# A streaming encoder layer on one core: the first modulation with weight blocks as the stationary operand

## The chip, the cores and the metric

One core of a Trainium2 chip runs the whole program. The metric is the device time of one execution in microseconds (us); lower is better.

## The reference

One layer of a hybrid encoder is applied to a prompt (512 tokens) and to a sample (64 tokens). What this case touches is the adaptive modulation at its start; the rest is cut.

```python
def trunk(x, c, states, params, block):
    ...
    mod = jax.nn.silu(c) @ w_ada[l] + b_ada[l]          # c: one row of 2048, for prompt and for sample
    sh1, sc1, g1, sh2, sc2, g2 = jnp.split(mod[:, None, :], N_MOD, axis=-1)
    h = rmsnorm(x, norm1[l]) * (1 + sc1) + sh1
    mix, ... = token_mixers(h, ..., w_in[l], ...)       # h @ w_in, two recurrences, out projection
    x = x + g1 * mix
    h = rmsnorm(x, norm2[l]) * (1 + sc2) + sh2
    f, s_f = conv_ffn(h, ...)
    x = x + g2 * f
```

All data are f32. `w_ada` is 2048 x 12288, six parts of 2048 columns; the first part is `sh1`, the second `sc1`. The head of the kernel needs these two only: a product of two rows (the prompt's c and the sample's) with 2048 x 4096 weights, 33.6 MB.

## The kernel before

**How it multiplies.** Large products are made from operands split in a high and a low half (tiles of type F32R): the high half is a rounded copy made by ScalarE (ACT, L649), the low half the rest, a subtraction on VectorE (DVE, L650). `wtile` loads a 512 KB tile of weights into `raw` or `hraw` over SyncE's queue (SP) and splits it to `wh` and `wl`. A wide product is three matmuls: high by high, low by high, high by low (`mm6`, L561 and L563), here with 128x128 weights stationary and 288 columns of the activations moving.

**The head.** `head` turns x to channel-major by TensorE transposes (L698), computes the rows' norms and their scaling (L725, L726), and makes the modulation of four 128-channel blocks at a time: `modulation(g)` for g = 0 to 3, each for `sc1` (mi = 1) and then `sh1` (mi = 0). So there are eight modulations of 2048 x 512 weights, each of eight tiles with two k (128 rows) in a tile. `modulation(0)` comes first, with the loads, turns and norms of x between its tiles. Then, for each g, `modulation(g + 1)` comes ahead of the work on the four blocks of g: their modulated h (`split_mod`), the narrow product (L877), and the first q and k products (L561 and L563 on `g` and `ps_k`, 64 wide matmuls per g with the narrow ones). TensorE keeps this order; the head ends with the last of these products. Behind it come the projections, the recurrences, the output projection and the FFN.

**The modulation before.** The columns of silu(c) are the stationary operand and the weights move, 512 columns at a time. `cst` holds for each k the high halves of both c's and the low halves (4 columns), padded with zeros to NW = 66. For six of the eight tiles the weights are split, and each k has two matmuls, by `wh` (L757) and by `wl` (L758). For the tiles at k0 = 4 and 12 the raw f32 weights move past the unsplit columns `cs4` (L753). The result lies in four rows of 512 columns; DVE copies it (`rw`, L760), four small matmuls (L763) turn it to columns and add the high and low rows, and `put_mod` adds the bias (L797).

The later modulations (parts 2 to 5) are made on VectorE by `ada_block`, whose sums are turned by matmuls with 128x128 stationary sums and one moving column (L826). These are not changed.

Of the kernel before, what the change touches and what calls it, by code (L numbers as in the profile page):

```python
# [8 lines left out]
F32 = mybir.dt.float32  # L9
F32R = mybir.dt.float32r  # L10
I32 = mybir.dt.int32
AF = mybir.ActivationFunctionType
ALU = mybir.AluOpType
# [3 lines left out]
P = 128  # L17
D = 2048
KD = 16
# [28 lines left out]
NW = 66  # L48
# [53 lines left out]
class Kern:  # L102
# [554 lines left out]
    def head(self, pool):  # L657
        nc, i = self.nc, self.i
        V, A, T = nc.vector, nc.scalar, nc.tensor
# [2 lines left out]
            next(vectors)  # L662

        self.ct = self.cp.tile([P, 2, KD], F32, name="ct")
        cst = pool.tile([P, KD, NW], F32R, tag="cst", bufs=1, name="cst")
        nc.gpsimd.memset(cst.bitcast(F32), 0.0)
        for s in range(2):
            A.activation(self.ct[:, s], self.vmap[f"c{s}"], AF.Silu)
        cs4 = pool.tile([P, KD, 4], F32, tag="cs4", bufs=1, name="cs4")
        nc.gpsimd.memset(cs4, 0.0)  # L670
        for s in range(2):
            V.tensor_copy(cs4[:, :, s], self.ct[:, s])
            A.activation(cst[:, :, s], self.ct[:, s], AF.Copy)
            V.tensor_tensor(cst[:, :, 2 + s], self.ct[:, s], cst[:, :, s].bitcast(F32), op=ALU.subtract)
        self.mod = self.cp.tile([P, 6, KD, 2], F32, name="mod")
# [61 lines left out]
        def hraw():  # L737
            if next(turns) == "r":
                return self.raw()
            return pool.tile([P, 1024], F32, tag="hraw", bufs=5, name=self.name("hraw"))  # L740

        def modulation(g, between=lambda: None):
            for mi in (1, 0):
                ps = self.bank()
                c0 = mi * D + g * 512
                for k0 in range(0, KD, 2):
                    between()
                    src = i["w_ada"][0, k0 * P:(k0 + 2) * P, c0:c0 + 512].rearrange("(k p) n -> p k n", p=P)
                    if k0 in (4, 12):
                        raw = hraw().rearrange("p (k n) -> p k n", k=2)  # L750
                        nc.sync.dma_start(raw, src)
                        for k in range(2):
                            T.matmul(ps[:4], cs4[:, k0 + k], raw[:, k], start=False, stop=False)  # L753
                        continue
                    wh, wl = self.wtile(src, hraw())
                    for k in range(2):
                        T.matmul(ps[:NW], cst[:, k0 + k], wh[:, k], start=(k0 + k == 0), stop=False)  # L757
                        T.matmul(ps[:NW], cst[:, k0 + k], wl[:, k], start=False, stop=(k0 + k == KD - 1))  # L758
                rw = pool.tile([4, 512], F32, tag="rw", bufs=1, name=self.name("rw"))
                V.tensor_copy(rw, ps[:4])  # L760
                pc = self.bank()
                for j in range(4):
                    T.matmul(pc[:, 2 * j:2 * j + 2], rw[:, j * P:(j + 1) * P], self.c["sel"][:4, 16:18], start=True, stop=True)  # L763
                self.put_mod(mi, 4 * g, pc)
                for _ in vectors:
                    pass
            self.scale_mod(s1, 1, "norm1", 4 * g)

        plan = [[] for _ in range(16)]
        for b in range(5):  # L770
            for f, at in ((x_load, 0), (x_turn, X_LAG), (x_norm, X_LAG + 1)):
                plan[X_AT[b] + at].append(lambda f=f, b=b: f(b))
        step = iter(plan)
        modulation(0, lambda: [f() for f in next(step)])
        rx = x_rows()
        self.ps_nar, self.ps_q0 = self.pgt(), self.pgt()
        for g in range(4):
            if g < 3:
                modulation(g + 1)
            ks = range(4 * g, 4 * g + 4)  # L780
            nar = self.narrow_w(pool, 4 * g)
            qw, kw = [self.split(pool, self.w_in(off)(4 * g, 4 * g + 4), "f", 512, 3) for off in (OFF_BQ, OFF_BK)]
            for k in ks:
                hh, hl = self.htiles(k)
                tmp = pool.tile([P, 2, HT], F32, tag="tmp", bufs=2, name=self.name("tmp"))
                self.split_mod(xT[:, k], rx, s1[:, k], self.mod[:, 0, k], hh, hl, tmp)
                nc.sync.dma_start(self.xs[k], xT[:, k])
                self.h.append((hh, hl))
                self.mm_narrow(k, nar[:, k % 4])
                for ps, w in ((self.ps_q0, qw), (ps_k0, kw)):  # L790
                    self.mm6(ps, w[0][:, k % 4], w[1][:, k % 4], self.h[k], k == 0, k == KD - 1)
        raw = self.xr()
        self.ps_k0 = raw[:, :2 * HT].rearrange("p (h t) -> p h t", h=2)
        V.tensor_copy(self.ps_k0, ps_k0[:, :, :HT])

    def put_mod(self, mi, k0, pc):
        self.nc.vector.tensor_tensor(  # L797
            self.mod[:, mi, k0:k0 + 4], pc[:, :8].rearrange("p (j s) -> p j s", s=2),
            self.vec("b_ada", mi * KD + k0, 4).unsqueeze(2).to_broadcast([P, 4, 2]), op=ALU.add)

    def scale_mod(self, out, mi, norm, k0, n=4):

# [1188 lines left out]
```

## Time and profile before

| | |
|---|---|
| time, median of 3 runs | 2870.66 us (2866.38 to 2871.43) |
| the profiled execution's own time | 2869.18 us |
| its span, first to last instruction | 2867.4 us |
| mean granted TensorE clock | 0.992 |
| TensorE (PE) busy | 2810.4 us, 98% |
| weight loads (PEld) busy | 2708.7 us, 94% |
| VectorE (DVE), ScalarE (ACT), GpSimd (POOL) busy | 80%, 47%, 11% |
| DMA | 399.80 MB, mean 139 GB/s |

PE and PEld are the two sides of TensorE: matmuls and the loads of their stationary operands, which overlap. A matmul's record contains its latency, so successive records overlap, and the distance of their starts tells the rate. The granted clock is the share of full speed that TensorE's clock was given. In a list of instructions "idle before <-X" is how long the engine stood still ahead of them and what ended that. Groups give busy time and the mean length of one in ns. A plain f32 matmul leaves two records, one of F32R operands one.

### The profile page before, as it was taken

What the parts mean: (1) busy time and instruction counts of PE and PEld (TensorE: products, weight loads), DVE (VectorE), ACT (ScalarE), POOL (GpSimd) and SP (SyncE); (2) the same over time, 40 slices, a digit from 0 to 9 for tenths busy, and PEclk for the clock granted to TensorE, in tenths of its full rate; (3) what the DMA queues carried; (4) which work ended last, traced back from release to release, by engine and by line L of the source; (5) the groups of instructions that cost most, each with busy time, mean ns of one, the idle gap of its engine ahead of it and who ended that gap; (6) DMA issues with size and microseconds to landing.
All of it is one profiled execution on the core that took longest, in us unless ns stands there. A gap on an engine that the chain in (4) does not pass through costs nothing.

```text
span 2867.4 us, 52042 instructions
## 1 busy us (share of the span) xinstructions
PE 2810.4 (98%) x20596; PEld 2708.7 (94%) x20596; DVE 2301.9 (80%) x3742; ACT 1355.0 (47%) x2379; POOL 320.6 (11%) x587
## 2 busy tenths in 40 slices
PE   7999999999999999999999999999999999999998
PEld 3599999999999999999999999999999999999997
DVE  5788878777778777468888888888887889999995
ACT  7574566544333333255444444444444464434453
POOL 0005432224310001001000000000000000000000
PEclk9999999999999999999999999999999999999999
DMA  9975555545455448433333333333333343443451
GB/s 308 306 209 148 157 149 161 158 140 152 129 166 172 146 131 251 123 119 102 102 101 102 108 106 108 102 108 108 101 101 105 105 150 114 123 127 118 126 169 67
DMA packets 522441, 399.80 MB, mean 139 GB/s; under 512 B 50793, under 2 KB 453956, under 8 KB 522196
## 3 DMA queue, kind: packets, MB, share of 16 engines
q1 hardware_dynamic: 516772, 385.79, 45.3%
q0 software_dynamic: 5424, 10.68, 1.2%
q8 instruction: 162, 2.65, 0.4%
q14 instruction: 83, 0.68, 0.1%
HBM read 356.24 MB, written 40.13 MB: 138 GB/s over the span
## 4 chain that ended last, share of the span: by engine, by line
PE 82%; DVE 9%; DMA 3%; ACT 3%; issue 2%; SPq 0%; POOL 0%; ACTq 0%; DVEq 0%
PE g L561 19%; PE g L563 10%; PE g L1373 9%; PE g L1374 8%; PE g L1375 8%; PE bank L1374 3%; PE bank L1373 3%; PE bank L1375 3%; DVE wl L1558 2%; PE g L1606 2%; PE g L1608 2%; PE g L1607 2%; DMA raw<-in_w_down_dram 1%; PE bank L162 1%; PE bank L826 1%
## 5 line engine op out<-in xcount | busy, mean ns | idle before, releaser
L1373 PE MATMUL g<-slot,wh 128*128 128x290 f32 x1760 | 534.2, 304 | 2.4 <-ACT p L1385 2.4
L1374 PE MATMUL g<-slot,wh 128*128 128x290 f32 x1760 | 526.6, 299 | 0.0
L1375 PE MATMUL g<-slot,wl 128*128 128x290 f32 x1760 | 520.9, 296 | 0.0
L561 PE MATMUL g<-hh,wh 128*128 128x288 f32 x1984 | 450.4, 307 | 2.4 <-ACT hh L1160 1.3
L561 PE MATMUL g<-hl,wh 128*128 128x288 f32 x1984 | 432.3, 298 | 0.0
L563 PE MATMUL g<-hh,wl 128*128 128x288 f32 x1984 | 432.0, 298 | 0.0
L1320 ACT ACTIVATE wh<-raw 128x1024 fp32r<-128x1024 f32 x176 | 186.8, 1061 | 393.1 <-PE g L1374 376.8
L1373 PEld LDWEIGHTS g<-slot,wh 128*128 128x128 f32 x1760 | 331.8, 189 | 16.9 <-ACT p L1385 11.3
L1375 PEld LDWEIGHTS g<-slot,wl 128*128 128x128 f32 x1760 | 337.2, 192 | 0.0
L1374 PEld LDWEIGHTS g<-slot,wh 128*128 128x128 f32 x1760 | 335.6, 191 | 0.1
L561 PEld LDWEIGHTS g<-hh,wh 128*128 128x128 f32 x1984 | 319.1, 190 | 5.6 <-ACT hh L1160 1.5
L561 PEld LDWEIGHTS g<-hl,wh 128*128 128x128 f32 x1984 | 321.3, 189 | 0.3
L563 PEld LDWEIGHTS g<-hh,wl 128*128 128x128 f32 x1984 | 319.6, 189 | 0.2 <-issue 0.2
L649 ACT ACTIVATE wh<-raw 128x1024 fp32r<-128x1024 f32 x163 | 172.6, 1059 | 309.1 <-PE g L561 272.6
L650 DVE TENSOR_TENSOR wl<-raw,wh 128x1024 fp32r<-128x1024 f32 x163 | 199.1, 1222 | 52.8 <-ACT wh L649 50.9
L820 DVE SCALAR_TENSOR_TENSOR acc<-xr,ct,acc 128x512 f32<-128x512 f32 x322 | 230.4, 751 | 1.5 <-DMA xr<-in_w_ada_dram 1.5
L1321 DVE TENSOR_TENSOR wl<-raw,wh 128x1024 fp32r<-128x1024 f32 x176 | 214.8, 1220 | 19.3 <-ACT wh L1320 19.2
L1606 PE MATMUL g<-slot,wh 128*128 128x288 f32 x760 | 224.8, 296 | 2.3 <-DVE slot L1623 1.1
L1608 PE MATMUL g<-slot,wl 128*128 128x288 f32 x760 | 224.4, 296 | 0.3 <-DVE wl L1558 0.3
L1607 PE MATMUL g<-slot,wh 128*128 128x288 f32 x760 | 224.4, 295 | 0.0
L1374 PE MATMUL bank<-slot,wh 128*128 128x290 f32 x704 | 210.3, 299 | 0.0
L1373 PE MATMUL bank<-slot,wh 128*128 128x290 f32 x704 | 209.6, 298 | 0.0
(416 smaller groups left out, 6083.0 us busy)
## 6 DMA issues: line engine op xcount, KB each, us to landing
raw<-in_w_up_dram SPq DMA_DIRECT2D x176, 512.0 KB, 4.0
raw<-in_w_in_dram SPq DMA_DIRECT2D x108, 512.0 KB, 3.9
xr<-in_w_ada_dram SPq DMA_DIRECT2D x86, 512.0 KB, 3.9
raw<-in_w_down_dram SPq DMA_DIRECT2D x76, 512.0 KB, 3.6
ax<-in_w_ada_dram SPq DMA_DIRECT2D x42, 512.0 KB, 3.7
hraw<-in_w_ada_dram SPq DMA_DIRECT2D x40, 512.0 KB, 9.5
raw<-in_w_out_dram SPq DMA_DIRECT2D x32, 512.0 KB, 4.3
raw<-in_w_ada_dram SPq DMA_DIRECT2D x24, 512.0 KB
```

Of the source, the lines that this page charges most:

```text
L561: T.matmul(ps[:, h if bank is None else bank, :n], wh, x[:, h, :n], start=f, stop=False)
L563: T.matmul(ps[:, h if bank is None else bank, :n], wl, ah[:, h, :n], start=False, stop=stop)
L650: nc.vector.tensor_tensor(lo[:, :n_], raw[:, :n_], hi[:, :n_].bitcast(F32), op=ALU.subtract)
L820: V.scalar_tensor_tensor(acc[s], w[:, k], col, acc[s], op0=ALU.mult, op1=ALU.add)
L1320: self.nc.scalar.activation(hi, src, AF.Copy)
L1321: self.nc.vector.tensor_tensor(lo, src, hi.bitcast(F32), op=ALU.subtract)
L1373: T.matmul(ps, wh[:, j], hi, start=(c < 3 and j == 0), stop=False, skip_group_check=True)
L1374: T.matmul(ps, wh[:, j], lo, start=False, stop=False, skip_group_check=True)
L1375: T.matmul(ps, wl[:, j], hi, start=False, stop=(j == NPAIR - 1), skip_group_check=True)
L1606: T.matmul(ps, wh[:, j, f], hi, start=(c < 3 and j == 0), stop=False, skip_group_check=True)
L1607: T.matmul(ps, wh[:, j, f], lo, start=False, stop=False, skip_group_check=True)
L1608: T.matmul(ps, wl[:, j, f], hi, start=False, stop=(j == n - 1), skip_group_check=True)
```

## The change

The operands of the modulation change places. A block of 128 x 128 weights is stationary, and the four columns of `cst` (high and low of both c's) move past it. Each k of a tile has four blocks for `wh` and four for `wl`, so a tile has 16 matmuls and a modulation 128. All of them add into one bank of 128 x 16 values: block j has four columns, the high and the low halves of c for prompt and sample. The result is already in columns, so the copy `rw` of four rows and the turn L763 go; two VectorE additions of 128 x 8 values add the high part to the bias and then the low part. All eight tiles are split; the raw f32 path, `cs4`, and the zero padding of `cst` go.

```diff
-        cst = pool.tile([P, KD, NW], F32R, tag="cst", bufs=1, name="cst")
-        nc.gpsimd.memset(cst.bitcast(F32), 0.0)
+        cst = pool.tile([P, KD, 4], F32R, tag="cst", bufs=1, name="cst")
...
-        cs4 = pool.tile([P, KD, 4], F32, tag="cs4", bufs=1, name="cs4")
-        nc.gpsimd.memset(cs4, 0.0)
         for s in range(2):
-            V.tensor_copy(cs4[:, :, s], self.ct[:, s])
...
             for mi in (1, 0):
-                ps = self.bank()
+                ps, n = self.bank(), 0
...
-                    if k0 in (4, 12):
-                        raw = hraw().rearrange("p (k n) -> p k n", k=2)
-                        nc.sync.dma_start(raw, src)
+                    for w in self.wtile(src, hraw()):
                         for k in range(2):
-                            T.matmul(ps[:4], cs4[:, k0 + k], raw[:, k], start=False, stop=False)
-                        continue
-                    wh, wl = self.wtile(src, hraw())
-                    for k in range(2):
-                        T.matmul(ps[:NW], cst[:, k0 + k], wh[:, k], start=(k0 + k == 0), stop=False)
-                        T.matmul(ps[:NW], cst[:, k0 + k], wl[:, k], start=False, stop=(k0 + k == KD - 1))
-                rw = pool.tile([4, 512], F32, tag="rw", bufs=1, name=self.name("rw"))
-                V.tensor_copy(rw, ps[:4])
-                pc = self.bank()
-                for j in range(4):
-                    T.matmul(pc[:, 2 * j:2 * j + 2], rw[:, j * P:(j + 1) * P], self.c["sel"][:4, 16:18], start=True, stop=True)
-                self.put_mod(mi, 4 * g, pc)
+                            for j in range(4):
+                                T.matmul(ps[:, 4 * j:4 * j + 4], w[:, k, j * P:(j + 1) * P], cst[:, k0 + k],
+                                         start=n == 0, stop=n == 16 * KD // 2 - 1, skip_group_check=True)
+                                n += 1
+                two = ps[:, :16].rearrange("p (j x s) -> p j x s", j=4, x=2)
+                rw = pool.tile([P, 4, 2], F32, tag="rw", bufs=2, name=self.name("rw"))
+                V.tensor_tensor(rw, two[:, :, 0], self.mod_bias(mi, 4 * g), op=ALU.add)
+                V.tensor_tensor(self.mod[:, mi, 4 * g:4 * g + 4], two[:, :, 1], rw, op=ALU.add)
```

`mod_bias` is the old bias operand of `put_mod`, now a function of its own.

The order of TensorE's program at two places follows. In a row, the line is followed by the operation, the bank it writes, the moving and the stationary operand's tile as the program names them (`wh` and `wl` the halves of a weight tile, `cst` and `cs` the columns of c, `hs` rows of x, `rw` the copied rows), and the shape. The new matmuls are L748, the transposes of x are L698 before and L694 now.

TensorE in the first modulation, from its start, before:

```order
L757 MATMUL bank_225<-wh_227,cst 66x512
L758 MATMUL bank_225<-wl_228,cst 66x512
L757 MATMUL bank_225<-wh_227,cst 66x512
L758 MATMUL bank_225<-wl_228,cst 66x512
L757 MATMUL bank_225<-wh_245,cst 66x512
L758 MATMUL bank_225<-wl_246,cst 66x512
L757 MATMUL bank_225<-wh_245,cst 66x512
L758 MATMUL bank_225<-wl_246,cst 66x512
L698 MATMUL g_276<-consts_95,hs_236 128x128 x4
L698 MATMUL g_282<-consts_95,hs_237 128x128 x4
L698 MATMUL g_288<-consts_95,hs_238 128x128 x4
L753 MATMUL bank_225<-raw_254,cs_211 4x512 x2
```

and now:

```order
L748 MATMUL bank_220<-cst,wh_222 128x4 x8
L748 MATMUL bank_220<-cst,wl_223 128x4 x8
L748 MATMUL bank_220<-cst,wh_252 128x4 x8
L748 MATMUL bank_220<-cst,wl_253 128x4 x8
L748 MATMUL bank_220<-cst,wh_274 128x4 x8
L748 MATMUL bank_220<-cst,wl_275 128x4 x8
L748 MATMUL bank_220<-cst,wh_304 128x4 x8
L694 MATMUL g_325<-consts_95,hs_243 128x128 x4
L748 MATMUL bank_220<-cst,wl_305 128x4 x8
L748 MATMUL bank_220<-cst,wh_350 128x4 x8
L694 MATMUL g_331<-consts_95,hs_244 128x128 x4
```

Each tile's four wide matmuls became sixteen narrow ones, and the first transposes of x stand behind three and a half tiles instead of two.

TensorE where the second modulation ends and the third begins, before:

```order
L753 MATMUL bank_427<-hraw_584,cs_211 4x512 x2
L757 MATMUL bank_427<-wh_589,cst 66x512
L758 MATMUL bank_427<-wl_590,cst 66x512
L757 MATMUL bank_427<-wh_589,cst 66x512
L758 MATMUL bank_427<-wl_590,cst 66x512
L763 MATMUL bank_600<-consts_95,rw_598 128x2 x4
L757 MATMUL bank_621<-wh_623,cst 66x512
```

and now:

```order
L748 MATMUL bank_525<-cst,wh_761 128x4 x8
L748 MATMUL bank_525<-cst,wl_762 128x4 x8
L748 MATMUL bank_525<-cst,wh_783 128x4 x8
L748 MATMUL bank_525<-cst,wl_784 128x4 x8
L748 MATMUL bank_822<-cst,wh_824 128x4 x8
```

The raw group and the turn L763 are gone from between the tiles, and the two modulations of g = 1 follow with no other TensorE work between them up to the first q and k products. From the narrow product's constants (before L890, now L882) on, TensorE's order is the same in both programs.

More of the change, by code (lines that the diff above doesn't have):

```diff
@@ L794, in head, with mod_bias @@
         V.tensor_copy(self.ps_k0, ps_k0[:, :, :HT])
+    def mod_bias(self, mi, k0):
+        return self.vec("b_ada", mi * KD + k0, 4).unsqueeze(2).to_broadcast([P, 4, 2])
     def put_mod(self, mi, k0, pc):
-        self.nc.vector.tensor_tensor(
-            self.mod[:, mi, k0:k0 + 4], pc[:, :8].rearrange("p (j s) -> p j s", s=2),
-            self.vec("b_ada", mi * KD + k0, 4).unsqueeze(2).to_broadcast([P, 4, 2]), op=ALU.add)
+        self.nc.vector.tensor_tensor(self.mod[:, mi, k0:k0 + 4], pc[:, :8].rearrange("p (j s) -> p j s", s=2),
+                                     self.mod_bias(mi, k0), op=ALU.add)
     def scale_mod(self, out, mi, norm, k0, n=4):
```

## The prediction

> **What bounds the kernel now.** I read the page's first lines, then busy time by stretch, then the timeline of the head, where every edit lies.
>
> ```profile
> span 2867.4 us, 52042 instructions
> PE 2810.4 (98%) x20596; PEld 2708.7 (94%) x20596; DVE 2301.9 (80%) x3742; ACT 1355.0 (47%) x2379; POOL 320.6 (11%) x587
> ```
>
> ```profile
> 11.20:58.20 47.00, 39.42 (x170) 20.92 (x170) 20.25 (x40) 34.50 (x74) 2.75 (x5) 0.85 0.92 310
> 58.20:160.00 101.80, 98.72 (x497) 61.35 (x496) 81.04 (x127) 57.98 (x84) 1.15 (x3) 1.00 0.92 303
> 160.00:175.00 15.00, 13.16 (x99) 12.59 (x100) 11.23 (x36) 9.79 (x21) 0.00 (x0) 1.00 0.61 181
> ```
>
> TensorE fills 98% of the span, so what it gains or loses in the head goes to the end almost one for one. A stretch's row has its length, the busy time of PE, PEld, DVE, ACT and POOL, the granted clock, the DMA share and GB/s. The head (to 160 us) is balanced: PE is busy 98.72 of 101.80 us while the transfers hold 92% of the DMA engines.
>
> ```profile
> 11.28 0.66 PE L757 MATMUL bank<-wh,cst 128*66 128x512 f32 x1 [0.54 <-DVE cst L674]
> 11.74 0.63 PE L758 MATMUL bank<-wl,cst 128*66 128x512 f32 x1
> 12.17 0.63 PE L757 MATMUL bank<-wh,cst 128*66 128x512 f32 x1
> ...
> 58.19 0.44 PE L757 MATMUL bank<-wh,cst 128*66 128x512 f32 x1
> ...
> 69.18 1.05 PE L763 MATMUL bank<-consts,rw 4*128 4x2 f32 x8 [0.78 <-DVE rw L760]
> 70.16 0.45 PE L757 MATMUL bank<-wh,cst 128*66 128x512 f32 x1
> 70.44 0.40 PE L758 MATMUL bank<-wl,cst 128*66 128x512 f32 x1
> 70.68 0.40 PE L757 MATMUL bank<-wh,cst 128*66 128x512 f32 x1
> ...
> 72.16 1.88 PE L753 MATMUL bank<-raw,cs 128*4 128x512 f32 x4
> 73.97 0.44 PE L757 MATMUL bank<-wh,cst 128*66 128x512 f32 x1
> ...
> 159.19 0.43 PE L561 MATMUL ps_k<-hl,fh 128*128 128x288 f32 x2
> 159.45 0.43 PE L563 MATMUL ps_k<-hh,fl 128*128 128x288 f32 x2
> ```
>
> Starts tell TensorE's rate, since a record contains its latency. At half clock (11.74 to 12.17) a 512-column matmul takes 0.43 us; at full clock 0.23 (70.44 to 70.68); a plain-f32 group L753 takes 1.81 (72.16 to 73.97); the wide 288-column matmuls take 0.1325 each (two from 159.19 to 159.45). The first two modulations end at 58.2, the head at 159.9.
>
> **The change, part by part.** Removed on TensorE: in each of eight modulations 24 matmuls, two L753 groups, and the turn L763, or 24 x 0.23 + 2 x 1.81 + 1.0 = 10.1 us; 81 us in all, as the counts of the head's groups (0 to 162 us) say:
>
> ```profile
> L757 PE MATMUL bank<-wh,cst 128*66 128x512 f32 x96 | 40.9, 426 | 0.5 <-DVE cst L674 0.5
> L758 PE MATMUL bank<-wl,cst 128*66 128x512 f32 x96 | 39.9, 415 | 0.6 <-DVE wl L650 0.6
> L753 PE MATMUL bank<-hraw,cs 128*4 128x512 f32 x32 | 15.0, 592 | 0.0
> L763 PE MATMUL bank<-consts,rw 4*128 4x2 f32 x64 | 8.4, 249 | 4.9 <-DVE rw L760 4.9
> L877 PE MATMUL g<-hl,nar 128*66 128x288 f32 x32 | 6.8, 294 | 0.0
> L698 PE MATMUL g<-consts,hs 128*128 128x128 f32 x64 | 9.1, 281 | 1.6 <-ACT xT L701 1.6
> L725 PE MATMUL g<-hs,consts 128*128 128x512 f32 x2 | 2.1, 1142 | 0.3 <-ACT xT L705 0.3
> L623 PE MATMUL bank<-consts,hs 88*128 88x88 f32 x3 | 1.2, 391 | 1.9 <-DVE cols L624 1.9
> ```
>
> Added: 16 k x 2 halves x 4 blocks = 128 matmuls in each modulation, 1024 in all, each with its own 128x128 load and only four moving columns. The nearest row is L826, 128x128 weights and one moving column:
>
> ```profile
> 408.21 1.84 PE L826 MATMUL bank<-consts,acc 128*128 128x1 f32 x16
> 409.92 0.52 PE L561 MATMUL g<-hl,wh 128*128 128x288 f32 x2
> ```
>
> ```profile
> L561 PEld LDWEIGHTS g<-hl,wh 128*128 128x128 f32 x13 | 2.1, 188 | 0.0
> L561 PEld LDWEIGHTS g<-hl,wh 128*128 128x128 f32 x4 | 1.1, 331 | 0.0
> L753 PEld LDWEIGHTS bank<-hraw,cs 128*4 128x4 f32 x32 | 2.1, 85 | 8.5 <-issue 8.5
> ```
>
> Sixteen in 1.71 us is 0.107 each, the load being the limit: a load record goes from 85 ns for 4 columns to 188 for 128, so 0.83 ns a column, 106 ns for the block. At full clock the 1024 would take 109 us, 28 more than the 81 removed. The 331 ns are the same load at half clock (410.7 to 414 us): 143 ns more, which covers the doubling of the 106. At half clock, then, 0.213 each: 218 us. Everything hangs on the clock.
>
> What the clock does under such a load the trace shows at two of the L826 bursts:
>
> ```profile
> 403.82:407.23 3.41, 3.41 (x28) 3.41 (x27) 3.03 (x13) 2.67 (x6) 0.56 (x1) 1.00 0.25 77
> 407.24:410.64 3.40, 3.22 (x27) 2.99 (x26) 1.05 (x5) 2.37 (x6) 0.00 (x0) 1.00 0.04 10
> 410.66:414.05 3.39, 3.39 (x17) 3.39 (x16) 3.39 (x7) 0.78 (x2) 0.67 (x1) 0.50 0.23 35
> 414.07:417.40 3.33, 3.33 (x28) 3.33 (x27) 3.33 (x6) 1.10 (x6) 0.00 (x0) 1.00 0.60 211
> ...
> 526.71:530.10 3.39, 3.39 (x33) 3.32 (x31) 1.53 (x3) 3.04 (x7) 2.92 (x7) 1.00 0.43 126
> 530.12:533.52 3.40, 3.40 (x16) 3.40 (x16) 3.31 (x7) 1.54 (x2) 2.85 (x8) 0.50 0.00 0
> ```
>
> The granted clock moves in steps of 3.41 us, and I cut the stretches there. From 407.24 PE is busy 3.22 of 3.40 us and loads weights 2.99, and still the next stretch is granted 0.50; from 526.71 PE is busy without a break, with the same result. Half of each of those stretches was one-column matmuls. So loading weights does not hold the clock, streamed columns do. One stretch of 288-column matmuls (410.66) brings it back. Other L826 bursts pass without a drop, but each is 1.7 us among wide matmuls; the change makes two modulations back to back, at least 27 us, or eight such stretches, in which columns stream for 4 of some 256 cycles. I take the half clock for all of them.
>
> The Trainium skill, "TensorE: Matmul & The Clock Gate", advises (last section) only to avoid idle gaps beyond about 3 us; by that alone the clock would hold here, since the loads leave no gap, and the sum would be that of the first rival, 2884; the 407.24 row speaks against it. The page's LDWEIGHTS section gives a load as columns/1.2 ns, 107 ns for a block whatever the gate does, and by it too the sum would be about 2884; the full-clock rows agree with it, the 331 ns do not.
>
> The sum for TensorE's head, at its new lengths:
> - start 11.3 as now (the c transfers set it; the dropped memsets and copies of c are worth nothing behind them, at most the 0.5 us wait);
> - 1024 x 0.213 = 218.4;
> - q, k and narrow: eight groups of 32 like the L877 row, 256 x 0.1325 = 33.9;
> - three times the wide block begins at half clock and needs on average 1.5 stretches (5.1 us, half lost) to get the clock back: +7.7; twice the next modulation then keeps it for about 3.9 us and does double work: -7.8;
> - turning x, now at half clock: 64 x 0.213 + 16 x 0.107 for the sample + 3.4 for the row scaling L725 and the vectors' transposes L623 = 18.7 (0.107 a transposition at full clock, by its 128 f32 columns; an estimate from the 0.83 ns a column);
> - waits for ScalarE and VectorE among these transposes, as now: 4 (1.6, 0.3 and 1.9 in the L698, L725 and L623 rows).
>
> Together 286.2, against 159.9: +126. Hidden under it:
>
> ```profile
> L650 DVE TENSOR_TENSOR wl<-hraw,wh 128x1024 fp32r<-128x1024 f32 x32 | 39.0, 1220 | 16.7 <-ACT wh L649 16.4
> L649 ACT ACTIVATE wh<-hraw 128x1024 fp32r<-128x1024 f32 x32 | 33.5, 1053 | 15.8 <-PE bank L757 8.4 <-DMA hraw<-in_w_ada_dram 7.0 <-PE bank L753 0.3
> L760 DVE COPY rw<-bank 4x512 f32<-4x512 f32 x8 | 5.4, 674 | 0.2
> ```
>
> Sixteen more splits cost DVE 19.5 us and ACT 16.8, less the copies L760; a tile of TensorE work now lasts 16 x 0.213 = 3.4 us against 1.22 and 1.05 of splitting, so both wait for TensorE; if that cover went (full clock, 1.7 us a tile), DVE's 81 + 15 us would still fit into the second stretch. The two small adds that replace L760 and L763 run while TensorE is in the next modulation's bank. DMA bytes are the same; the raw tiles of k0 4 and 12 are now freed by the split instead of by a matmul, and the x rows, q/k weights and stores of x change places on SP's queue with w_ada tiles. At 3.4 us a 512 KB tile the queue runs ahead of TensorE, where now it is the near limit, so none of these moves is late. Behind the head TensorE's order is unchanged, so nothing is given back there.
>
> Against the profiled execution's own 2869.18 us that is **2995**; the median of the three runs is 1.5 us above that execution, which changes nothing.
>
> **Ends of the unknown costs.** The one price without a row is a load-bound matmul at half clock. Its lower end is the full-clock 0.107 (rival 1), its upper end 0.24, which 288 columns need at half clock: +27. I stay at 0.213, twice the L826 spacing, since that row is the nearest by kind. Inside the forecast the clock may also be lifted by the transposes, or be kept longer behind the wide blocks; nine stretches of 3.41 us at double rate would be -30.
>
> **Rivals.**
> 1. The clock holds. For it: most L826 bursts cost no clock. Against: the 407.24 and 526.71 rows. The first pair still ends near 59 by its transfers, then 768 x 0.107 + 33.9 = 116: the head ends at 175, +15, **2884**.
> 2. The clock swings: full in part of the stretches. Anything from 2884 to 2960, about **2925**.
> 3. A matmul with four columns is run in two passes like the f32 groups, whose 32 calls make 64 L753 records. Against: the F32R operands of L757 make one record a call. 1024 more loads: +218, **3213**.
> 4. Not slower: blocks load in one cycle a column, half of the 0.107. Break-even is a spacing of 0.080 us, where 256 new matmuls a stage equal the removed 20.3. At 0.055 and full clock the transfers bind; they already hold 92%, so the gain is at most the 8% of 102 us: -8, **2861**. Against: the 1.71 us of L826.
>
> **Chances.** Half clock (forecast) 0.81; rival 1 0.08, rival 2 0.05, rival 3 0.03, rival 4 0.03. The forecast's own range is 2965 to 3022; to hold 8 in 10 I reach down into rival 2, 2950 to 3024. Within 0.2% (5.7 us, about what a measurement of this kernel can tell from no change) I put 0.02, a third of rival 4 and a small part of rival 1; faster 0.02, the rest of rival 4; slower 0.96.
>
> **What would show it.** Right: PEclk 0.5 through nearly all of 11 to 275 us, L748 starts 0.21 us apart, load records near 330 ns, DMA share in the head near half, wide matmuls of the head slow for some 20 at a time, the head's end near 286 and an unchanged tail. Wrong: a granted clock of 1.0 in the modulations (rival 1), twice 1024 L748 records (rival 3), or TensorE waiting on wl or DMA between tiles.

## The result and the profile after

The changed kernel takes 3006.6 us (median of five runs, 3002.75 to 3010.47), against 2868.45 us (2866.38 to 2871.43) before: 1.0479 times as long, 95% interval 1.0465 to 1.0494. The profiled execution took 3010.47 us, its span is 3008.7, 141.3 more than before.

The page's first lines after, then stretches of the head (columns as before):

```profile
span 3008.7 us, 53505 instructions
PE 2950.6 (98%) x21300; PEld 2899.6 (96%) x21300; DVE 2318.7 (77%) x3756; ACT 1372.2 (46%) x2395; POOL 315.8 (10%) x585
```

```profile
11.20:100.00 88.80, 78.36 (x360) 74.22 (x360) 25.34 (x47) 40.89 (x82) 2.74 (x5) 1.00 0.55 173
100.00:160.00 60.00, 60.00 (x293) 59.95 (x293) 30.97 (x48) 22.32 (x31) 0.00 (x0) 1.00 0.56 174
...
155.80:165.90 10.10, 10.10 (x85) 10.10 (x83) 7.05 (x13) 4.86 (x8) 0.32 (x1) 1.00 0.53 156
166.00:217.00 51.00, 51.00 (x239) 50.94 (x239) 20.16 (x29) 15.47 (x19) 0.00 (x0) 0.50 0.55 169
217.20:227.30 10.10, 10.10 (x84) 10.10 (x83) 7.95 (x14) 5.89 (x8) 0.78 (x2) 1.00 0.50 157
227.40:278.50 51.10, 51.10 (x239) 51.03 (x239) 20.16 (x29) 15.19 (x19) 0.00 (x0) 0.50 0.44 131
```

From 166 to 217 us TensorE is busy in all of the 51.00 us and loads weights in 50.94 of them, and its clock is granted at half. The full clock comes for 10 us with the wide products and goes again. (The first clock record of this trace begins at 155.7 us; the 1.00 ahead of it means only that nothing was recorded. There the starts must tell.) The timeline of TensorE at four places:

```profile
11.18 1.87 PE L748 MATMUL bank<-cst,wh 128*128 128x4 f32 x8 [0.48 <-DVE cst L670]
...
96.92 1.84 PE L748 MATMUL bank<-cst,wh 128*128 128x4 f32 x8
98.63 1.84 PE L748 MATMUL bank<-cst,wl 128*128 128x4 f32 x8
...
151.53 0.83 PE L561 MATMUL ps_k<-hh,fh 128*128 128x288 f32 x2
...
161.94 0.95 PE L748 MATMUL bank<-cst,wh 128*128 128x4 f32 x8
162.75 1.03 PE L748 MATMUL bank<-cst,wl 128*128 128x4 f32 x8
163.64 1.03 PE L748 MATMUL bank<-cst,wh 128*128 128x4 f32 x8
...
166.66 1.84 PE L748 MATMUL bank<-cst,wl 128*128 128x4 f32 x8
168.37 1.84 PE L748 MATMUL bank<-cst,wh 128*128 128x4 f32 x8
...
292.81 0.42 PE L563 MATMUL ps_k<-hh,fl 128*128 128x288 f32 x2
```

Eight of the new matmuls take 1.71 us (96.92 to 98.63), 0.213 each; at full clock, just behind the wide products, 0.89 (162.75 to 163.64), 0.112 each; from 166 on 0.213 again. The first pair of modulations, with the transposes of x among its matmuls, lasts from 11.18 to 96.92 us, the second pair, 256 matmuls, to 151.53. The head ends at 293.2 in place of 159.9.

The loads themselves, between 100 and 150 us of the changed kernel:

```profile
L748 PEld LDWEIGHTS bank<-cst,wh 128*128 128x128 f32 x120 | 27.4, 333 | 0.0
```

A load's record lasts 333 ns, where the loads of such blocks last 192 to 193 at full clock (161.9 to 165.9 us).

### The profile page after: what moved, and what is told of

It is laid out like the page before. It is cut to its first block, busy times and chain, and to the rows that moved or that the text cites. A ratio compares the mean times of both kernels' runs of the same rounds, so it can differ in the third digit from the quotient of the medians.

```text
span 3008.7 us, 53505 instructions
## 1 busy us (share of the span) xinstructions
PE 2950.6 (98%) x21300; PEld 2899.6 (96%) x21300; DVE 2318.7 (77%) x3756; ACT 1372.2 (46%) x2395; POOL 315.8 (10%) x585
## 4 chain that ended last, share of the span: by engine, by line
PE 80%; DVE 11%; DMA 4%; ACT 3%; issue 2%; SPq 0%; POOL 0%; ACTq 0%; DVEq 0%; POOLq 0%
PE g L561 18%; PE g L563 9%; PE g L1365 8%; PE g L1366 8%; PE g L1367 8%; PE bank L748 7%; PE bank L1366 3%; PE bank L1365 3%; PE bank L1367 3%; DVE wl L1550 2%; DMA raw<-in_w_down_dram 1%; PE g L1598 1%; PE g L1600 1%; DVE acc L812 1%; PE g L1599 1%
## 5 line engine op out<-in xcount | busy, mean ns | idle before, releaser
L1312 ACT ACTIVATE wh<-raw 128x1024 fp32r<-128x1024 f32 x176 | 186.7, 1061 | 392.3 <-PE g L1366 388.1
L649 ACT ACTIVATE wh<-raw 128x1024 fp32r<-128x1024 f32 x171 | 180.8, 1058 | 332.6 <-PE g L561 267.9
L650 DVE TENSOR_TENSOR wl<-raw,wh 128x1024 fp32r<-128x1024 f32 x171 | 209.0, 1223 | 65.8 <-ACT wh L649 52.3
L1313 DVE TENSOR_TENSOR wl<-raw,wh 128x1024 fp32r<-128x1024 f32 x176 | 214.5, 1219 | 19.8 <-ACT wh L1312 19.7
```

The lines of the kernel that those rows point to most:

```text
L650: nc.vector.tensor_tensor(lo[:, :n_], raw[:, :n_], hi[:, :n_].bitcast(F32), op=ALU.subtract)
L1313: self.nc.vector.tensor_tensor(lo, src, hi.bitcast(F32), op=ALU.subtract)
```

## The experiments

The theory: a stretch in which TensorE only loads weights does not keep its clock, however busy it is, and at half clock the load is the price, 0.213 us. The rivals: the new matmuls are slow by their form; the extra splits cost; the first pair's transposes and waits cost.

**The columns repeated.** The four columns are read 32 times over, so each matmul streams 128; loads, order and result stay.

```diff
-   T.matmul(ps[:, 4 * j:4 * j + 4], w[:, k, j * P:(j + 1) * P], cst[:, k0 + k],
+   T.matmul(ps[:, 128 * j:128 * j + 128].rearrange("p (r c) -> p r c", c=4), w[:, k, j * P:(j + 1) * P],
+            cst[:, k0 + k].unsqueeze(1).to_broadcast([P, 32, 4]),
...
```

> The four moving columns are repeated 32 times (128 columns, the copies' results unused); the 1024 weight loads, their order and all else stay as in the changed kernel. Theory of the clock (stretches of mere loading lose the full clock): 128 columns stream for 53 of the 107 ns between starts, so the clock stays at 1.0, starts stand 0.107 us apart, the head ends near 180 and the time is about 2885 to 2895 us. Rival, the form itself (a load of an F32R block with a short matmul takes 0.213 us whatever the clock): starts stay at 0.213 us and the time at 3007 or above. Rival, short F32R matmuls stream at several cycles a column: the clock is 1.0 but starts stand 0.2 us or more apart, about 3000.

It took 2935.3 us, 1.023 (1.0215 to 1.0245) of before: 71 us of the loss gone with more work on TensorE, but 45 us short of what I expected. The stretches say why (first and second row half and full clock), and the timeline shows where the clock is lost:

```profile
77.00:114.00 37.00, 37.00 (x174) 36.98 (x174) 18.36 (x24) 12.66 (x15) 0.00 (x0) 0.50 0.77 265
114.30:148.20 33.90, 31.41 (x269) 31.08 (x269) 21.91 (x33) 16.60 (x22) 0.32 (x1) 1.00 0.55 171
```

```profile
139.96 1.06 PE L748 MATMUL bank<-cst,wl 128*128 128x128 f32 x8
140.85 1.06 PE L748 MATMUL bank<-cst,wh 128*128 128x128 f32 x8
...
147.42 1.19 PE L748 MATMUL bank<-cst,wh 128*128 128x128 f32 x8 [2.34 <-ACT wh L649]
148.68 1.55 PE L748 MATMUL bank<-cst,wl 128*128 128x128 f32 x6
```

Behind the wide products the block matmuls ran 0.112 us apart at full clock for 26 us, until a wait of 2.34 us for a split tile. Then the clock halved and did not come back under the same matmuls, just as from 76.6 us to the wide products at 111.7. All four losses of this head come right behind waits: 2.18 us (lost at 35.7), 1.19 and 0.26 (at 76.6), 2.34 (at 148.3) and 1.23 (at 192.7). So neither the form nor the streaming of short matmuls is slow (both rivals fall in this one trace, where one and the same instruction takes 0.112 and 0.213). Streaming in half of the time kept the clock here as long as nothing had to be waited for, and did not regain it; I had not counted on the second.

**Fewer copies.** 64 and 96 columns. The shares of time that follow are estimates: in the kernel before 512 columns take 0.43 us at half clock (11.74 to 12.17), which makes 0.84 ns a column, so about 0.42 at full clock. Of the 112 ns between starts 64 columns are then 24%, 96 columns 36% and 128 columns 48%.

> The same with 16 copies (64 columns, 27 of 107 ns, a quarter of the time). Theory of the clock, with the limit near a third of the time as in the windows of the kernel before: the clock is lost as with four columns, 3007 us. If the limit lies lower, or if any stream will do: 2885 to 2895. Rival of the form: 3007 with a granted clock of 1.0 in the head.

> 24 copies, 96 columns, 40 of 112 ns or 36% of the time at full clock. Theory with a limit between a quarter (64 columns lost the clock one window after the wide products) and a half (128 kept it until a wait): this one lies close to it; if the limit is above 36% the clock is lost as with 64, about 2973 to 3007; if below, it is kept for tens of us behind the wide products as with 128, about 2935 to 2960.

One run each: 2972.9 us, 34 below the 3007 that the theory gave for 64 columns, and 2978.1, within what it gave for a lost clock. Behind the wide products, 64 columns and then 96 columns:

```profile
135.20:145.40 10.20, 10.20 (x84) 10.20 (x84) 5.49 (x11) 3.80 (x7) 0.32 (x1) 1.00 0.14 44
145.50:196.60 51.10, 51.10 (x240) 51.08 (x240) 23.37 (x30) 18.05 (x22) 0.00 (x0) 0.50 0.64 193
```

```profile
132.70:142.90 10.20, 10.20 (x86) 10.20 (x84) 5.12 (x11) 4.36 (x7) 0.32 (x1) 1.00 0.05 19
142.95:194.00 51.05, 51.05 (x239) 51.01 (x239) 23.90 (x31) 17.75 (x20) 0.00 (x0) 0.50 0.59 174
```

Both lose the clock without any wait, as four columns do. For these matmuls the limit for keeping it lies between 36% and 48% of the time in streaming. The number of matmuls does not decide: in a stretch of 3.41 us at full clock there are 30 or 31 of them with 4, 64, 96, 128 and 256 columns alike.

In the profiled executions the head ends at 273.0 us with 64 columns and at 270.0 with 96, some 20 us before the changed kernel's. They had the full clock for 14 and 20 us of the first 61, where transposes stand among the blocks, and waited 8 and 6 us less. The rest of their lead lies behind the head.

**Columns for all of the time.** 64 copies, 256 columns a matmul, the four blocks in two banks; the rest as above.

```diff
-   ps, n = self.bank(), 0
+   pss, n = [self.bank(), self.bank()], 0
...
+   T.matmul(pss[j // 2][:, 256 * (j % 2):256 * (j % 2) + 256].rearrange("p (r c) -> p r c", c=4), w[:, k, j * P:(j + 1) * P],
+            cst[:, k0 + k].unsqueeze(1).to_broadcast([P, 64, 4]),
...
```

> The four columns repeated 64 times (256 columns a matmul, blocks 0 and 1 in one bank, 2 and 3 in another, so the next modulation waits for the additions). In the run with 128 columns the same loads ran 0.112 us apart from 121 to 147 us at full clock, lost it at a wait for data of 2.3 us and did not get it back. Theory of the clock: 256 columns stream for nearly all of the 0.112 us, so the clock is granted soon after the start and comes back within two windows of any wait; the first pair ends near 60, then 768 x 0.112 + 34 + 6 for the banks: the head ends near 186 and the time is 2885 to 2900 us. Rival, the loads themselves slow each other or the transfers at this rate: the clock is 1.0 and starts stand well over 0.112 us apart, or waits fill the head, above 2915.

2890.8 us, 1.0077 (1.0062 to 1.0092) of before. Stretches and timeline:

```profile
11.20:60.00 48.80, 46.40 (x364) 44.33 (x365) 25.10 (x50) 40.17 (x80) 2.74 (x5) 0.97 0.95 319
60.00:180.00 120.00, 116.40 (x976) 115.14 (x975) 93.12 (x149) 68.61 (x93) 1.10 (x3) 0.99 0.77 247
```

```profile
100.40 1.05 PE L748 MATMUL bank<-cst,wl 128*128 128x256 f32 x8
101.29 1.05 PE L748 MATMUL bank<-cst,wh 128*128 128x256 f32 x8
...
183.88 0.42 PE L563 MATMUL ps_k<-hh,fl 128*128 128x288 f32 x2
```

With the clock held but for two stretches of 3.41 us behind waits, the same 1024 loads, each with 64 times the columns, end the head at 184.3, against 293.2. So about 109 us of the head's 133 are the clock. The other 24 lie in the last three pairs (the first ends at 57.8, before at 58.2) and are about what the block form costs at full clock: 768 matmuls at 0.112 us against the break-even of 0.080 are 25 us. A wait of 2.9 us for the two banks is in them too; what the transfers hide was not measured apart.

**One pair alone.** The kernel before, with blocks and four columns in the last pair of modulations (g = 3) only. They read their columns from a copy without padding, `cs8`.

```diff
-   modulation(g + 1)
+   (blocks if g + 1 in (3,) else modulation)(g + 1)      # blocks: the changed modulation
```

> The kernel before, with the change made in the last pair of modulations (g = 3) alone, 256 of the 1024 block matmuls, four columns each. Theory: the pair starts at full clock behind wide products, loses it after 4 to 7 us, and takes 50.5 us in place of some 22.5; the wide products behind it start at half clock (+2.5): +31, 2895 to 2905 us. Rival, a cost of the first pair alone (its waits among the transposes): no more than +10, below 2880.

2902.0 us, 1.0121 (1.0104 to 1.0138), 34 us more than before; the head ends at 191.5, 31.6 us later, with a quarter of the new matmuls. The clock goes as it does in the changed kernel, by its stretches:

```profile
104.80:125.10 20.30, 20.30 (x129) 15.69 (x127) 14.11 (x23) 10.40 (x16) 0.32 (x1) 1.00 0.89 303
125.30:176.30 51.00, 51.00 (x238) 50.98 (x239) 20.31 (x30) 15.30 (x20) 0.00 (x0) 0.50 0.50 158
```

In the changed kernel the last three pairs and their wide products take 196.3 us (from 96.92) in place of 101.7, which is 31.5 more for each pair, as here. The first pair takes 85.7 in place of 46.9, 38.8 more. So the loss is no matter of the first pair's transposes and waits, which add some 7 us.

**The splits alone.** The kernel before, with the raw f32 path at k0 = 4 and 12 taken out (with `cs4`, which it alone read) and all tiles split.

```diff
-                    if k0 in (4, 12):
-                        raw = hraw().rearrange("p (k n) -> p k n", k=2)
-                        nc.sync.dma_start(raw, src)
-                        for k in range(2):
-                            T.matmul(ps[:4], cs4[:, k0 + k], raw[:, k], start=False, stop=False)
-                        continue
```

> The kernel before with one part of the change alone: the tiles at k0 = 4 and 12 are split too, the weights still move. TensorE's work falls by 1.7 us a modulation (4 matmuls of 0.23 us for two f32 groups of 1.81 us and two more pairs), 14 us in all, VectorE's and ScalarE's rises by 19.5 and 16.8 us. Theory: the split is no part of the loss, the clock stays, and the transfers (92% of the head) let through at most 8 us: 2860 to 2869. Rival, the added splits cost time: above 2875.

2871.7 us, 1.0012 (1.0003 to 1.0021): no loss to speak of and no gain, between the 2860 to 2869 that I expected and the rival's 2875. Head stretches of before and of this kernel:

```profile
11.20:160.00 148.80, 138.15 (x665) 82.27 (x665) 101.29 (x166) 92.47 (x158) 3.90 (x8) 0.95 0.92 305
```

```profile
11.20:160.00 148.80, 128.80 (x631) 85.17 (x632) 115.77 (x182) 105.94 (x173) 3.90 (x8) 0.92 0.89 296
```

```profile
L749 PE MATMUL bank<-wl,cst 128*66 128x512 f32 x128 | 56.8, 444 | 8.8 <-DVE wl L650 8.4 <-DVE ms L710 0.3
```

TensorE's work fell by 9 us, and its waits grew: for the low halves from DVE (8.4 us, L749 is L758 of before) and for x from ScalarE (3.9 against 1.6). It also had less of its clock, 0.92 against 0.95 in the head, so the clock did not stay quite as I expected. In the profiled execution, the slowest of the twelve, the head ends at 164.9, 5 us later than before. That the raw f32 groups cost nothing because the transfers limit the head is my reading; no run tests it alone.

**The bursts behind the head.** 64 columns of ones in place of one in L826, in the changed kernel and in the one before.

```diff
-   T.matmul(pc[:, 2 * j + s:2 * j + s + 1], acc[s][:, j * P:(j + 1) * P], self.c["ones"][:, 0:1],
+   T.matmul(pc[:, 64 * (2 * j + s):64 * (2 * j + s) + 64], acc[s][:, j * P:(j + 1) * P], self.c["ones"][:, 0:64],
...
-   self.put_mod(blk // 4, 4 * (blk % 4), pc)
+   self.put_mod(blk // 4, 4 * (blk % 4), pc[:, 0:512:64])
```

> The changed kernel with 64 moving columns of ones in place of one in the turns of the later modulations (L826 of the kernel before), 16 bursts behind the head. The tail of the changed kernel was 8 us longer than before with the same order of work. Theory: more of these bursts happened to fill half of a clock window and lost the next one; with 64 columns none does, and the time falls by 5 to 9 us, to 2998 to 3002. Rival: the tail is longer for another reason (transfers, VectorE): 3005 to 3008.

> The kernel before with 64 columns of ones in place of one in the turns of the later modulations. In the changed kernel the same edit did not shorten the tail, since half-clock windows came at other places. If two windows behind these bursts were all that it cost here: -3.4 us, 2865 to 2868. If the waits of the tail decide, no difference: 2866 to 2873.

3008.5 us, 1.0485 (1.0469 to 1.0500), and 2875.6 us, 1.0030 (1.0020 to 1.0039): nothing gained, and the kernel before even lost 0.3%, more than either of its ranges has. My theory of the tail falls in its simple form. A table of the tails (from the head's last product to the span's end) says more. Half-clock time is added up from the trace's clock records, without the idle end of the span; waits are TensorE's idle time ahead of matmuls.

| kernel | head ends | tail | at half clock | waits | tail - half of it - waits |
|---|---|---|---|---|---|
| before | 159.9 | 2707.5 | 20.5 | 22.8 | 2674.5 |
| changed | 293.2 | 2715.5 | 30.7 | 24.2 | 2675.9 |
| 64 columns | 273.0 | 2698.1 | 10.2 | 19.5 | 2673.4 |
| 96 columns | 270.0 | 2706.0 | 23.9 | 20.4 | 2673.7 |
| 128 columns | 222.4 | 2704.0 | 23.9 | 18.7 | 2673.3 |
| 256 columns | 184.3 | 2702.3 | 17.1 | 19.7 | 2674.1 |
| last pair | 191.5 | 2705.1 | 17.1 | 20.8 | 2675.8 |
| splits alone | 164.9 | 2710.3 | 27.3 | 21.5 | 2675.2 |
| changed, wide L826 | 294.7 | 2713.6 | 30.7 | 27.1 | 2671.2 |
| before, wide L826 | 161.7 | 2711.9 | 17.1 | 30.1 | 2673.3 |

The last column is the same within 5 us in all of them. So the tail's work did not change, and its length follows the half-clock stretches and waits, which fall differently in each kernel. In the changed kernel with wide bursts the clock was lost elsewhere, at 390 us for 17 us in a row, among waits of 2.65 and 4.25 us for VectorE. Why the wide bursts made the waits longer (30.1 against 22.8 in the kernel before) stays open.

No experiment points to a version that beats the kernel before: blocks need 16 x 0.112 = 1.8 us a tile even at full clock, the moving form 4 x 0.23 = 0.92.

## Why the prediction was right

Forecast 2995 (2950 to 3024), measured 3006.6, slower by half clock as forecast. In the profiled executions the loss is 141 us against the forecast's 126; 7 of the difference lie in the head and 8 in the tail. By its terms:

- **The price at half clock**, taken as twice the L826 spacing, 0.213: measured 0.213, and 54.6 us for the second pair's 256. The load's record, 331 ns forecast from another line's, is 333. Some luck is in it. In the trace the first step of the burst at 408.21 is 0.03 us and the other 15 are 0.112, so 0.107 is an average that a long row of loads does not reach. Twice 0.112 would have made the 1024 matmuls 229 us, 11 more than measured: the spacing at half clock is 1.9 times that at full clock, and not twice.
- **That mere loading loses the clock**, read from two windows before: shown by the changed kernel's 166 to 217 us and, by changing the streamed columns alone (with 256 the banks too), by the runs with 64 to 256 columns.
- **Getting it back and carrying it over**: forecast 5.1 us of half-clock wide products and 3.9 us of full-clock blocks, near cancelling. Measured: the first wide block lasts 10.4 us (151.53 to 161.94; 11.0 in the sum), and the blocks behind it keep the clock for 4.0 us (to 165.96).
- **DMA near half in the head**: 0.44 to 0.56.
- **Waits among the transposes, 4 us**: mis-sized. By the timeline they are 10.4:

```profile
33.92 1.87 PE L748 MATMUL bank<-cst,wh 128*128 128x4 f32 x8 [1.08 <-ACT wh L649]
...
42.11 1.86 PE L748 MATMUL bank<-cst,wh 128*128 128x4 f32 x8 [2.24 <-ACT wh L649]
...
55.80 1.97 PE L694 MATMUL g<-consts,hs 128*128 128x128 f32 x8 [1.53 <-ACT xT L697]
...
61.44 0.54 PE L623 MATMUL bank<-consts,hs 88*128 88x88 f32 x2 [3.35 <-DVE cols L624]
62.95 0.41 PE L623 MATMUL bank<-consts,hs 88*128 88x88 f32 x1 [0.97 <-DVE cols L624]
...
83.25 1.86 PE L748 MATMUL bank<-cst,wh 128*128 128x4 f32 x8 [1.26 <-ACT wh L649]
```

That is 6.4 of the 7.0 us by which the head missed, 293.2 against 286.2. (The first pair as a whole lasts 85.7 us where the sum has 77.2; 2 us of that lie in smaller steps that no run takes apart, and what follows comes out 1.4 us shorter than the sum.) I took over only the waits of three rows of before, and left out a fourth, 1.1 us for `cols`; three of the six are for ScalarE's split of a weight tile, which shares ScalarE with the turning and squaring of x.
- **An unchanged tail**: its work is, its length is not, +7.9 us: 5 of half clock, 1.4 of waits, the rest within the scatter of the table.
- **Rival 1** (the clock holds, 2884) was the right size for a case that did not happen: the run with 256 columns makes it happen and measures 2890.8. A rule on gaps alone, which the prediction weighed as the Trainium skill's ("TensorE: Matmul & The Clock Gate", last section), would have missed the changed kernel: there was no gap from 155.8 to 217 us, and at 166 the clock fell to half.

## What to carry to other kernels

Count a matmul with few moving columns by its load, and ask what share of the time columns stream: here at 36% and below TensorE lost its full clock while it was 100% busy, and each of these matmuls then cost 0.213 us in place of 0.112. The shares are estimates from this one kernel. Before turning a product round so that the weights are stationary, compare 128-column loads per tile with columns streamed per tile; here the turned form loses even at full clock (1.8 against 0.92 us a tile). A busy share of 98% in both kernels showed none of this; the granted clock and the distance of starts did.

## What the runs showed of the hardware

- The clock has a memory: 128 columns in 112 ns (48%, estimated) kept the full clock for 26 us, until a wait, and did not regain it in 35 us at half, where they also stream half of the time. Wide products (288 columns) regained it 2.5 to 6.4 us after the first of them, in the runs with 128 and 4 columns.
- At full clock the load-bound spacing is 0.112 us, the same with 4, 64, 96, 128 and 256 columns; at half clock it is 0.213 (4, 96 and 128 columns).
- A trace's clock column says nothing ahead of its first record (155.7 us in the changed kernel).
